# Final norm of an encoder trunk: token sums on output partitions, root and reciprocal on one column per 128 tokens

## The chip, the cores and the metric

One core of a Trainium2 chip runs the whole program. The metric is the device time of one execution in microseconds; of several runs the median is given. TensorE (PE) multiplies matrices into PSUM banks of 128 partitions x 512 fp32, VectorE (DVE), ScalarE (ACT) and GpSimd (POOL) work on 128 partitions, and SyncE (SP) issues most of the transfers.

## The reference

The reference is an encoder trunk with two layers over 1040 tokens (16 learned ones, 1024 given) of width 1024. Each layer has a norm, an input projection, a gated delta rule in both directions beside a short convolution, an output projection, a second norm and a SwiGLU network. Only its end matters here:

```python
def rmsnorm(x, w):
    xf = x.astype(jnp.float32)
    y = xf * lax.rsqrt(jnp.mean(xf * xf, axis=-1, keepdims=True) + RMS_EPS)
    return (y * w.astype(jnp.float32)).astype(x.dtype)
...
    h = rmsnorm(h, final_norm_w)
    return h[:, N_META:]
```

So every token is divided by the root of the mean square of its 1024 channels, and every channel is multiplied by a weight.

## The kernel before

Activations lie with channels on partitions: the residual is eight rows `hr[m]` of 128 channels x 1040 tokens, in two tiles `hb[0]` and `hb[1]` of four rows each. A sum over channels is therefore a sum over partitions and over the eight rows. Dense products are made in `dense`: for each chunk of tokens a PSUM bank takes three matmuls for each 128 channels of input (high and low parts of both operands), then an eviction runs, here `add_h`, which adds the bank to `hr[m]` on VectorE (line 905).

The last piece of the program is the rest of the last layer's down projection, with four blocks of input, so 12 matmuls for each product. It runs over three chunks of tokens, `FIN = [(16, 528), (528, 784), (784, 1040)]`, and inside a chunk over the eight rows. For each row there are the product and its eviction, `add_sq` (square on ScalarE, lines 181 and 187, sum over rows into `ss` on VectorE, line 188), and the multiplication by the norm's weight on ScalarE (line 1422). `ss`, whose tile is called `rstd` in the profile, then holds for each token and partition a sum over eight channels.

At the end of each chunk `finish_rstd` multiplies a matrix of ones with `ss` (line 196), so that every partition of bank `a` holds the full sum of each token, takes the root of the mean on ScalarE (line 197) and the reciprocal on VectorE (line 198), both over all tokens of the chunk on all 128 partitions. Then the eight rows are multiplied with the result (line 1426), the even ones on VectorE and the odd ones on GpSimd, and after every two rows SyncE issues a transfer to `out` (line 1427). The program ends with the last of these.

The products of this stage take their banks from `pwide`, which goes round `acc` (three banks) and `f` (two). Banks `a` (one) and `b` (two) are free for the norm. The order of the instructions on each engine is laid down when the program is built, by a planner that follows the order of the program text as a priority and puts later work ahead where it expects an engine to be free. On the chip each engine then runs its own queue in that order, with semaphores between engines.

Names that the change uses: `ident` is a 128x128 identity, `ones` a 128x128 matrix of ones, both fp32; `t2k` gives a tile of 128 x 4 x 128 fp32 from a ring of five; `bank("b")` gives a PSUM bank; `tt` is a product or sum of two tensors on VectorE, `ptt` the same on GpSimd; `st` is a ring of two small tiles, which the delta rule used before.

Of the kernel before, what the change touches and what calls it, by code (L numbers as in the profile page):

```python
# [7 lines left out]
F32 = mybir.dt.float32  # L8
F32R = mybir.dt.float32r
BF16 = mybir.dt.bfloat16  # L10
AF = mybir.ActivationFunctionType
ALU = mybir.AluOpType

DEPTH = 2
D = 1024
# [27 lines left out]
def trunk(ctx: ExitStack, tc: tile.TileContext, xT, w_in, w_ba, w_out, w_gu, w_dn,  # L43
          par_d, alog_d, dtb_d, cst_d, eye_d, out):
    nc = tc.nc
    sb = ctx.enter_context(tc.tile_pool(name="sb", bufs=1))
# [5 lines left out]
    def nm(p):  # L52
        cnt[0] += 1
        return f"{p}_{cnt[0]}"
# [4 lines left out]
    def row(tag, dt=F32, bufs=1):  # L59
        return sb.tile([128, L], dt, tag=tag, bufs=bufs, name=nm(tag))  # L60

    def t2k(tag):
        return sb.tile([128, 4, 128], F32, tag="ck2", bufs=5, name=nm(tag))
# [4 lines left out]
    def bank(tag):  # L68
        return psp.tile([128, 512], F32, tag=tag, bufs={"acc": 3, "a": 1, "f": 2, "b": 2}[tag], name=nm("p" + tag))
# [28 lines left out]
    mm = nc.tensor.matmul  # L98
    act = nc.scalar.activation
    tt = nc.vector.tensor_tensor  # L100
    stt = nc.vector.scalar_tensor_tensor
    ts = nc.vector.tensor_scalar
    ptt = nc.gpsimd.tensor_tensor
# [8 lines left out]
    ones = sb.tile([128, 128], F32, name="ones")  # L112
# [19 lines left out]
    def wload(src, nk):  # L132

        res = []
        step = min(nk, WK)
        for k0 in range(0, nk, step):
            kk = min(step, nk - k0)
            hi = wp.tile([128, WK, 128], F32R, tag="whi", name=nm("whi"))
            lo = wp.tile([128, WK, 128], F32R, tag="wlo", name=nm("wlo"))
            wsplit(src[:, k0:k0 + kk, :], hi[:, 0:kk, :], lo[:, 0:kk, :])  # L140
            for k in range(kk):
                res.append((hi[:, k, :], lo[:, k, :]))
        return res

    def dense(ws, xs, chunks, evac, pool=None):

        for (n0, n1) in chunks:
            n = n1 - n0
            ps = (pool or pacc)()
            K = len(xs)  # L150
            here = tc.cur_priority
            if mmp[0] is not None:
                at_prio(mmp[0])
            for k in range(K):
                (wh, wl), (xh, xl) = ws[k], xs[k]
                mm(ps[:, :n], wh, xh[:, n0:n1], start=(k == 0), stop=False)  # L156
                mm(ps[:, :n], wh, xl[:, n0:n1], start=False, stop=False)  # L157
                mm(ps[:, :n], wl, xh[:, n0:n1], start=False, stop=(k == K - 1))  # L158
            if mmp[0] is not None:
                mmp[0] = tc.cur_priority  # L160
                at_prio(here)
            here = tc.cur_priority
            if evp[0] is not None:
                at_prio(evp[0])
            evac(ps[:, :n], n0, n1)
            if evp[0] is not None:
                evp[0] = tc.cur_priority
                at_prio(here)
            for q in (jobs, jobs2, jobs3):
                f = q.pop(0) if q else None  # L170
                if f is not None:
                    f()
# [6 lines left out]
    def add_sq(h, ss, first, add=nc.vector.tensor_tensor, dve=False, prev=None):  # L179
        if first:  # L180
            after(act(out=ss, in_=h, func=AF.Square), prev)
        else:
            sq = c4k("sq")[:, 0:h.shape[1]]
            if dve:
                after(tt(out=sq, in0=h, in1=h, op=ALU.mult), prev)
            else:
                after(act(out=sq, in_=h, func=AF.Square), prev)
            add(out=ss, in0=ss, in1=sq, op=ALU.add)

    cols = {}  # L190

    def finish_rstd(ss, chunks):
        for j, (n0, n1) in enumerate(chunks):
            n = n1 - n0
            ps = bank("abb"[j])
            mm(ps[:, :n], ones, ss[:, n0:n1], start=True, stop=True)
            act(out=ss[:, n0:n1], in_=ps[:, :n], func=AF.Sqrt, scale=1.0 / D, bias=cols["eps"])
            nc.vector.reciprocal(out=ss[:, n0:n1], in_=ss[:, n0:n1])  # L198

    def finish_bc(ss, n0, n1, dst, ps=None):  # L200

# [25 lines left out]
    ss = row("rstd")  # L227
# [29 lines left out]
    ident = sb.tile([128, 128], F32, name="ident")  # L257
# [21 lines left out]
    for l in range(DEPTH):  # L279
# [607 lines left out]
        chunks = ochunks  # L887
        hb = [big(X[0][0]), big(X[0][1])]
        hr = [hb[m // 4][:, m % 4, :] for m in range(KT)]
# [13 lines left out]
        def add_h(m, then=None):  # L903
            def f(ps, n0, n1):
                tt(out=hr[m][:, n0:n1], in0=ps, in1=hr[m][:, n0:n1], op=ALU.add)
                if then is not None:
                    then(n0, n1)
            return f

        def next_norm(m, xm, wcol, ss):  # L910
            def f(n0, n1):
                split_scaled(hr[m][:, n0:n1], wcol, xm[0][:, n0:n1], xm[1][:, n0:n1])
                add_sq(hr[m][:, n0:n1], ss[:, n0:n1], m == 0)
            return f
# [25 lines left out]
        ss = row("rstd")  # L940
# [316 lines left out]
        for f in range(FT):  # L1257
# [21 lines left out]
            ps = {}  # L1279
# [63 lines left out]
        hr = [hb[m // 4][:, m % 4, :] for m in range(KT)]  # L1343
# [34 lines left out]
        for u, (p, b, m) in enumerate(UNITS):  # L1378
            if b == 1 and p in FIRST:
                dh, z = FIRST[p]  # L1380
                q = 4 * dh + m
# [12 lines left out]
            for j in range(NJ):  # L1394
                ps = bks[m, j]
                cs = slice(CW * j, CW * j + CW)
                for k in range(3):
                    th, tl = t_slot(3 * (u // 4) + k)
                    st = p in ("P2", "P5", "P1") and b == 0 and k == 0
# [4 lines left out]
                if b == NBK - 1:  # L1404
                    dh, z, op = TO[p]
# [5 lines left out]
        ss = row("rstd")  # L1411
        if not last:
            for m in range(KT):
                then = next_norm(m, x[m], par[:, (l + 1) * P_L + P_N1 + m:(l + 1) * P_L + P_N1 + m + 1], ss)
                dense(pre.pop(("dn", m)) if m < 2 else wload(w_dn[l, m, :, 0:NF, :], NF), rest, chunks, add_h(m, then), pwide)
                dma(hd[m], hr[m])
        else:
            for (n0, n1) in FIN:
                for m in range(KT):
                    dense(wds[m], rest, [(n0, n1)], add_h(m), pwide)  # L1420
                    add_sq(hr[m][:, n0:n1], ss[:, n0:n1], m == 0)
                    act(out=hr[m][:, n0:n1], in_=hr[m][:, n0:n1], func=AF.Copy, scale=par[:, 2 * P_L + m:2 * P_L + m + 1])
                finish_rstd(ss, [(n0, n1)])
                for m in range(0, KT, 2):
                    for q in (m, m + 1):
                        (tt, ptt)[q % 2](out=hr[q][:, n0:n1], in0=hr[q][:, n0:n1], in1=ss[:, n0:n1], op=ALU.mult)  # L1426
                    dma(out[m:m + 2, :, n0 - 16:n1 - 16].rearrange("m p t -> p m t"), hb[m // 4][:, m % 4:m % 4 + 2, n0:n1])
        if not last:
            finish_bc(ss, 0, L, rsd[1])
# [74 lines left out]
```

## Time and profile before

| | us |
|---|---|
| three runs | 2576.59, 2575.36, 2570.45 |
| median | 2575.36 |
| profiled execution, its own time | 2574.08 |
| its span on the core | 2572.3 |
| TensorE busy | 2493.8 |
| VectorE busy | 1722.1 |
| ScalarE busy | 1046.3 |
| GpSimd busy | 246.3 |

The span runs from the first to the last instruction on the core; the execution's own time is 1.8 us longer. The mean granted clock of TensorE over the span is 0.987 of full speed. In rows of the timeline stand the start, the duration, the engine, the line, the operation with the tiles that it writes and reads, the count, and in brackets the idle time of the engine before it with what ended it. Neighbouring instructions of one engine overlap by their fill and drain, so the distance of two starts is what an instruction costs in a row of equals.

### The profile page before, as it was taken

To read this page: it belongs to the slowest core of one execution; us is meant where nothing else is said; L and a number is where in the kernel's file an instruction comes from. 1 tells how busy PE (TensorE), PEld (TensorE's weight loads), DVE (VectorE), ACT (ScalarE), POOL (GpSimd) and SP (SyncE) were. 2 spreads that over 40 slices of the span, in tenths; PEclk is the share of its full clock that TensorE was granted. 3 is DMA by queue.
4 is the path that set the end of the run, shared out by engine and by line. 5 is a ranking of instruction groups with operands and counts; after the bars stand their busy time and mean duration, and the time that the engine had idled before them with its cause. 6 is when DMAs were issued, how large, how long until landed. Compare 5 with 4: busy or idle time off the path is not lost.

```text
span 2572.3 us, 44715 instructions
## 1 busy us (share of the span) xinstructions
PE 2493.8 (97%) x17442; PEld 2285.1 (89%) x17442; DVE 1722.1 (67%) x3055; ACT 1046.3 (41%) x1933; POOL 246.3 (10%) x264
## 2 busy tenths in 40 slices
PE   8989999999999999989999989999999999999997
PEld 6989999999999999989998878999888888887786
DVE  4678523549877777778656785235698767768866
ACT  5564323426333333434445633323453333334444
POOL 2041212200000000000011302222000000000002
PEclk9999999999999999999999999999999999999998
DMA  3458355524432222663323573456344222238431
GB/s 124 125 166 269 117 174 165 180 73 148 145 110 90 90 93 79 234 208 119 93 93 125 184 243 126 139 178 208 105 143 145 97 94 90 86 108 300 150 114 66
DMA packets 213567, 359.99 MB, mean 140 GB/s; under 512 B 25268, under 2 KB 87676, under 8 KB 213356
## 3 DMA queue, kind: packets, MB, share of 16 engines
q1 hardware_dynamic: 180684, 310.69, 36.8%
q10 hardware_dynamic: 30496, 42.09, 5.1%
q0 software_dynamic: 2176, 4.36, 0.6%
q8 instruction: 137, 2.24, 0.4%
q14 instruction: 74, 0.61, 0.1%
HBM read 266.60 MB, written 90.46 MB: 139 GB/s over the span
## 4 chain that ended last, share of the span: by engine, by line
PE 76%; DVE 9%; DMA 8%; issue 2%; ACT 2%; POOL 1%; ACTq 0%; SPq 0%; POOLq 0%; DVEq 0%
PE pacc L156 7%; PE pacc L158 7%; PE pacc L157 7%; PE pacc L1063 4%; PE pacc L1061 4%; PE pacc L1062 4%; PE pb L1063 3%; PE pb L1061 3%; PE pb L1062 3%; PE pf L1061 3%; PE pf L1063 3%; PE pf L1062 3%; PE pacc L1401 2%; PE pacc L1403 2%; PE pacc L1402 2%
## 5 line engine op out<-in xcount | busy, mean ns | idle before, releaser
L156 PE MATMUL pacc<-a,whi 128*128 128x346 f32 (+1 forms) x808 | 266.0, 332 | 14.2 <-ACT whi L129 9.6
L158 PE MATMUL pacc<-a,wlo 128*128 128x346 f32 (+1 forms) x808 | 266.4, 331 | 0.7 <-POOL wlo L130 0.7
L130 POOL TENSOR_TENSOR wlo<-raw,whi 128x512 fp32r<-128x512 f32 x92 | 123.1, 1340 | 1427.3 <-ACT whi L129 1357.1
L156 PE MATMUL pacc<-b,whi 128*128 128x346 f32 (+2 forms) x672 | 235.2, 351 | 0.5 <-DVE a L730 0.5
L158 PE MATMUL pacc<-b,wlo 128*128 128x346 f32 (+2 forms) x672 | 232.5, 348 | 1.0 <-DVE wlo L130 1.0
L157 PE MATMUL pacc<-a,whi 128*128 128x346 f32 (+1 forms) x688 | 227.0, 330 | 1.7 <-DVE a L900 1.7
L129 ACT ACTIVATE whi<-raw 128x512 fp32r<-128x512 f32 x168 | 105.2, 629 | 251.1 <-PE pacc L157 191.0
L157 PE MATMUL pacc<-b,whi 128*128 128x346 f32 (+2 forms) x580 | 201.5, 347 | 0.3 <-DVE b L900 0.3
L156 PEld LDWEIGHTS pacc<-a,whi 128*128 128x128 f32 x808 | 154.6, 192 | 19.8 <-ACT whi L129 10.7
L158 PEld LDWEIGHTS pacc<-a,wlo 128*128 128x128 f32 x808 | 155.8, 193 | 3.0 <-issue 1.5
L158 PEld LDWEIGHTS pacc<-b,wlo 128*128 128x128 f32 x672 | 126.9, 189 | 11.1 <-DVE wlo L130 1.3
L156 PEld LDWEIGHTS pacc<-b,whi 128*128 128x128 f32 x672 | 127.1, 189 | 10.4 <-issue 2.2
L157 PEld LDWEIGHTS pacc<-a,whi 128*128 128x128 f32 x688 | 132.0, 192 | 4.7 <-DVE a L900 2.0
L157 PEld LDWEIGHTS pacc<-b,whi 128*128 128x128 f32 x580 | 109.7, 189 | 8.8 <-issue 1.3
L1043 ACT ACTIVATE whi<-rw 128x512 fp32r<-128x512 f32 x92 | 58.1, 631 | 128.6 <-DVE rw L1271 29.8
L1043 ACT ACTIVATE b<-rw 128x512 fp32r<-128x512 f32 x64 | 40.2, 632 | 143.7 <-PE pacc L1062 47.3
L295 DVE TENSOR_TENSOR a<-pacc,rstd 128x346 f32<-128x346 f32 (+2 forms) x59 | 32.6, 553 | 83.7 <-PE pacc L158 83.6
L1426 POOL TENSOR_TENSOR b<-b,rstd 128x256 f32<-128x256 f32 (+1 forms) x12 | 13.3, 1137 | 726.2 <-DVE rstd L198 726.2
L1043 ACT ACTIVATE a<-rw 128x512 fp32r<-128x512 f32 x64 | 40.2, 629 | 101.6 <-PE pacc L1062 72.2
L295 DVE TENSOR_TENSOR b<-pacc,rstd 128x346 f32<-128x346 f32 (+1 forms) x63 | 32.2, 512 | 70.8 <-PE pacc L158 70.7
L1044 DVE TENSOR_TENSOR wlo<-rw,whi 128x512 fp32r<-128x512 f32 x92 | 62.9, 685 | 6.3 <-ACT whi L1043 5.6
L130 DVE TENSOR_TENSOR wlo<-raw,whi 128x512 fp32r<-128x512 f32 x76 | 52.3, 688 | 15.8 <-ACT whi L129 15.2
(969 smaller groups left out, 8041.7 us busy)
## 6 DMA issues: line engine op xcount, KB each, us to landing
raw<-in_w_in SPq DMA_DIRECT2D x112, 256.0 KB
raw<-in_w_gu SPq DMA_DIRECT2D x104, 256.0 KB
rw<-in_w_gu SPq DMA_DIRECT2D x88, 256.0 KB
rec<-aqd SPq DMA_DIRECT2D x62, 256.0 KB
rec<-vkd SPq DMA_DIRECT2D x61, 256.0 KB
rw<-in_w_dn SPq DMA_DIRECT2D x70, 192.0 KB
raw<-in_w_out SPq DMA_DIRECT2D x48, 256.0 KB
b<-ad SPq DMA_DIRECT2D x45, 260.0 KB
```

Source lines behind the costliest of these rows:

```text
L129: act(out=hi, in_=raw[:, 0:kk, :], func=AF.Copy)
L130: (tt if lov[0] else ptt)(out=lo, in0=raw[:, 0:kk, :], in1=hi.bitcast(F32), op=ALU.subtract)
L156: mm(ps[:, :n], wh, xh[:, n0:n1], start=(k == 0), stop=False)
L157: mm(ps[:, :n], wh, xl[:, n0:n1], start=False, stop=False)
L158: mm(ps[:, :n], wl, xh[:, n0:n1], start=False, stop=(k == K - 1))
L295: tt(out=t[:, n0:n1], in0=ps, in1=rstd[:, n0:n1], op=ALU.mult)
L1043: act(out=hi, in_=src, func=AF.Copy)
L1044: tt(out=lo, in0=src, in1=hi.bitcast(F32), op=ALU.subtract)
L1061: mm(ps[:, :CW], w[0][:, k, :], th[:, cs], start=first and k == 0, stop=False, skip_group_check=True)
L1062: mm(ps[:, :CW], w[0][:, k, :], tl[:, cs], start=False, stop=False, skip_group_check=True)
L1063: mm(ps[:, :CW], w[1][:, k, :], th[:, cs], start=False, stop=stop and k == nk - 1, skip_group_check=True)
L1401: mm(ps[:, :CW], wh[:, k, :], th[:, cs], start=st, stop=False, skip_group_check=True)
```

## The change

`finish_rstd` is replaced by `final_scale`. For each 128 tokens of the chunk a matmul takes the 128x128 block of `ss` as weights and one column of ones as the moving side; its output has the tokens on partitions and is one column of a bank, so a chunk has four columns or two. Root and reciprocal run on these columns. One product on VectorE of the identity with the columns, each spread over 128 places, gives for each 128 tokens a diagonal matrix, and a matmul with ones as weights spreads each diagonal over all partitions of a bank. All eight rows are then multiplied on VectorE with this bank, which stays in PSUM; GpSimd has no part any more. The transfers stay as they were.

```diff
-    def finish_rstd(ss, chunks):
-        for j, (n0, n1) in enumerate(chunks):
-            n = n1 - n0
-            ps = bank("abb"[j])
-            mm(ps[:, :n], ones, ss[:, n0:n1], start=True, stop=True)
-            act(out=ss[:, n0:n1], in_=ps[:, :n], func=AF.Sqrt, scale=1.0 / D, bias=cols["eps"])
-            nc.vector.reciprocal(out=ss[:, n0:n1], in_=ss[:, n0:n1])
+    def final_scale(ss, n0, n1):
+
+        nt = (n1 - n0) // 128
+        ps = bank("a")
+        for j in range(nt):
+            mm(ps[:, j:j + 1], ss[:, n0 + 128 * j:n0 + 128 * j + 128], ones[:, 0:1], start=True, stop=True)
+        r = sb.tile([128, 4], F32, tag="st", bufs=2, name=nm("rt"))[:, 0:nt]
+        act(out=r, in_=ps[:, 0:nt], func=AF.Sqrt, scale=1.0 / D, bias=cols["eps"])
+        nc.vector.reciprocal(out=r, in_=r)
+        dg = t2k("dg")[:, 0:nt, :]
+        tt(out=dg, in0=ident.unsqueeze(1).to_broadcast([128, nt, 128]), in1=r.unsqueeze(2).to_broadcast([128, nt, 128]), op=ALU.mult)
+        bc = bank("b")
+        for j in range(nt):
+            mm(bc[:, 128 * j:128 * j + 128], ones, dg[:, j, :], start=True, stop=True)
+        return bc[:, 0:n1 - n0]
...
-                finish_rstd(ss, [(n0, n1)])
+                bc = final_scale(ss, n0, n1)
                 for m in range(0, KT, 2):
                     for q in (m, m + 1):
-                        (tt, ptt)[q % 2](out=hr[q][:, n0:n1], in0=hr[q][:, n0:n1], in1=ss[:, n0:n1], op=ALU.mult)
+                        tt(out=hr[q][:, n0:n1], in0=bc, in1=hr[q][:, n0:n1], op=ALU.mult)
```

## The prediction

> **What bounds the kernel now.** I read the page first, then busy time by stretches for the tail, then the timeline of each engine there, because the change touches only the final norm and that lies in the last 40 us.
>
> ```profile
> span 2572.3 us, 44715 instructions
> PE 2493.8 (97%) x17442; PEld 2285.1 (89%) x17442; DVE 1722.1 (67%) x3055; ACT 1046.3 (41%) x1933; POOL 246.3 (10%) x264
> ...
> 2541.00:2548.00 7.00, 4.89 (x42) 4.69 (x41) 7.00 (x8) 1.55 (x4) 5.94 (x4) 1.00 0.56 217
> 2548.00:2556.00 8.00, 7.63 (x62) 7.38 (x62) 7.04 (x17) 6.71 (x17) 0.00 (x0) 1.00 0.20 74
> 2556.00:2561.00 5.00, 0.00 (x0) 0.00 (x0) 4.82 (x9) 1.80 (x4) 3.37 (x4) 0.67 0.53 177
> 2561.00:2564.50 3.50, 1.22 (x2) 0.50 (x2) 1.71 (x1) 0.53 (x2) 0.00 (x0) 0.50 0.14 47
> ```
>
> In the stretches the columns are length, busy PE, PEld, DVE, ACT and POOL, granted PE clock, DMA share and GB/s. Over the whole span TensorE is the bound (97%). In the tail it is not: from 2541 to 2548 VectorE is busy 7.00 of 7.00 us and TensorE only 4.89, and after 2556 TensorE has nothing left but the last sums. So the tail, some 35 us, is priced on VectorE and on the chain at its end.
>
> ```profile
> 2528.96 0.40 PE L158 MATMUL pacc<-b,a3f 128*128 128x512 f32 x1
> 2534.14 1.02 PE L196 MATMUL pa<-rstd,ones 128*128 128x512 f32 x2
> 2535.07 1.28 ACT L197 ACT_TABLE_LOAD   x1
> 2536.37 0.69 ACT L197 ACTIVATE rstd<-pa,epsc 128x512 f32<-128x512 f32 x1
> 2537.09 3.35 DVE L198 RECIPROCAL rstd<-rstd 128x512 f32<-128x512 f32 x1 [0.75 <-ACT rstd L197]
> 2541.30 6.19 DVE L1426 TENSOR_TENSOR b<-b,rstd 128x512 f32<-128x512 f32 x4
> 2547.88 0.39 PE L156 MATMUL pf<-b,a 128*128 128x256 f32 x1 [2.11 <-DVE b L905]
> 2551.72 0.59 PE L196 MATMUL pa<-rstd,ones 128*128 128x256 f32 x2
> 2554.24 1.75 DVE L198 RECIPROCAL rstd<-rstd 128x256 f32<-128x256 f32 x1
> 2555.36 0.28 PE L158 MATMUL pacc<-b,a3f 128*128 128x256 f32 x1
> 2556.52 3.21 DVE L1426 TENSOR_TENSOR b<-b,rstd 128x256 f32<-128x256 f32 x4
> 2559.65 0.41 DVE L905 TENSOR_TENSOR b<-pacc,b 128x256 f32<-128x256 f32 x1
> 2559.98 0.98 DVE L188 TENSOR_TENSOR rstd<-rstd,sq 128x256 f32<-128x256 f32 x2
> 2561.02 1.22 PE L196 MATMUL pa<-rstd,ones 128*128 128x256 f32 x2 [5.39 <-DVE rstd L188]
> 2562.28 0.47 ACT L197 ACTIVATE rstd<-pa,epsc 128x256 f32<-128x256 f32 x1 [1.23 <-PE pa L196]
> 2562.79 1.75 DVE L198 RECIPROCAL rstd<-rstd 128x256 f32<-128x256 f32 x1 [1.82 <-ACT rstd L197]
> 2564.57 3.01 DVE L1426 TENSOR_TENSOR b<-b,rstd 128x256 f32<-128x256 f32 x4
> 2564.62 3.55 POOL L1426 TENSOR_TENSOR b<-b,rstd 128x256 f32<-128x256 f32 x4 [5.17 <-DVE rstd L198]
> ```
>
> Three costs are to be read here. The first chunk's reciprocal (3.35) and four multiplications (6.19) block VectorE for most of 10.4 us; TensorE runs out of free banks and waits 2.11 us at 2547.88 for an eviction (L905). The last dense matmul is over at 2555.64 (2555.36 + 0.28), but its eviction starts only at 2559.65, because the second chunk's reciprocal and multiplications stand ahead of it on VectorE. And from the last eviction (over at 2560.06) the chain square, add, sums, root, reciprocal, multiplications is serial; the last multiplication ends at 2568.17 and the span at 2572.3, 4.1 us later.
>
> **The sums.** Each sum over the channels was one matmul with ones as weights and 512 or 256 columns. Now the sums are weights, 128 tokens at a time, with one moving column: four or two such matmuls. The nearest rows have weights of 128x128 and 36 to 72 columns, in the same two passes.
>
> ```profile
> 83.66 0.31 PE L387 MATMUL pb<-g,utri 128*128 128x36 f32 x2
> 83.80 0.39 PE L387 MATMUL pb<-g,ltri 128*128 128x36 f32 x2
> 84.02 0.42 PE L388 MATMUL pb<-g,ones 128*128 128x72 f32 x2
> 84.25 0.41 PE L158 MATMUL pacc<-a,wlo 128*128 128x348 f32 x1
> 2535.13 0.28 PE L157 MATMUL pf<-b,a 128*128 128x256 f32 x1
> ```
>
> Starts are 0.14 to 0.23 us apart, so four take 0.6 to 0.9; the one of 512 columns held TensorE from 2534.14 to 2535.13, 0.99. I book nothing here (bounds -0.4 to 0).
>
> **Root and reciprocal.** They now run over four or two elements per partition.
>
> ```profile
> L867 ACT ACTIVATE st<-st x17: 204/206/226, 460.4 to 1839.1; 128x4 f32<-128x4 f32 x16, 16x4 f32<-16x4 f32 x1
> L868 DVE RECIPROCAL st<-st x17: 164/178/179, 460.7 to 1839.4; 128x4 f32<-128x4 f32 x16, 16x4 f32<-16x4 f32 x1
> L869 DVE TENSOR_TENSOR a3f<-a3f,st x8: 678/692/2267, 1763.0 to 1839.6; 128x512 f32<-128x512 f32 x8
> ```
>
> The root falls from 0.69 or 0.47 to 0.21, the reciprocal from 3.35 or 1.75 to 0.18. The table load of 1.28 stays where it is. The scaled identity is new on VectorE: 0.69 for 512 columns (the product with a broadcast column, L869), about 0.42 for 256 (as L905).
>
> **The spread.** Its matmuls, ones against the scaled identity, have as many columns in all as the old sums: 0.99 for the first chunk and, from 2551.72, about 0.5 for the second. In the last chunk the old sums took 1.22 with the clock at 0.50, against 0.59 at 1.00, so I book 1.25 there. The clock fell during the idle of TensorE: a mean of 0.67 over 2556 to 2561 means that it was at half for 3.3 of the 5.0 us, so from about 2557.7, some 2.05 us after the last dense matmul; the idle of 2.11 before 2547.88 left it at 1.00. The Trainium skill (TensorE: Matmul & The Clock Gate, "What's actually happening") gives half rate after an idle window of about 3.4 us, in windows that run freely. The trace agrees that idleness halves the clock, and its 2.05 us was enough. By that rule a last chain that starts within a window of the last matmul would run at full rate, and this chunk's spread would take 0.6 and its sums 0.6.
>
> **The multiplications.** All eight are on VectorE now, with one operand in PSUM and GpSimd silent.
>
> ```profile
> L1426 POOL TENSOR_TENSOR b<-b,rstd x12: 777/906/1751, 2540.6 to 2567.3; 128x256 f32<-128x256 f32 x8, 128x512 f32<-128x512 f32 x4
> 2477.02 0.68 DVE L1407 TENSOR_TENSOR b<-pa,b 128x512 f32<-128x512 f32 x1
> 2477.62 0.55 DVE L1182 TENSOR_TENSOR wlo<-rw,whi 128x384 fp32r<-128x384 f32 x1
> 2548.08 0.41 DVE L905 TENSOR_TENSOR b<-pacc,b 128x256 f32<-128x256 f32 x1
> 2548.41 0.41 DVE L905 TENSOR_TENSOR b<-pf,b 128x256 f32<-128x256 f32 x1
> ```
>
> Beside GpSimd four on VectorE took 6.19 (1.55 each). A product from PSUM, back to back, has its successor start after 0.60 (2477.02 to 2477.62) and, at 256 columns, 0.33 (2548.08 to 2548.41). Eight are 4.8 and 2.7: halving the engines is a gain, since each was slowed by the other. VectorE's block for the first chunk goes from 3.35 + 6.19 = 9.54 to 0.18 + 0.69 + 4.8 = 5.7.
>
> **The sum.** TensorE: the wait of 2.11 goes, since five banks hold five products of 1.4 to 1.5 us (12 matmuls each; 62 took 7.63) and the block is 5.7; the spreads add 1.0 + 0.5. The last dense matmul then ends at 2555.64 - 2.11 + 1.5 = 2555.0. Its eviction is over at 2555.5, and with the old 0.90 from there through square and add (2560.06 to 2560.96) the sums are ready at 2556.4 instead of 2560.96: 4.6 us earlier at best. What is late next is the second chunk's scale. Its spread needs root, reciprocal and identity first, two hops more than before, and in the old order its multiplications came between the last two evictions; I expect them behind the last eviction. Ahead of the last add they hold it for the rest of 2.7 us: only 2.4 earlier. Behind that add they hold the last reciprocal, which is not ready before 2556.4 + 1.28 + 0.26 = 2557.9, until 2559.1, a loss of 1.2: 3.4 earlier. The last chain: root -0.24, reciprocal -1.57, identity +0.46, spread +1.25, end after the first multiplication -0.7. That last term is bounded by -0.85 (eight multiplications end at 2.7 instead of 3.55) and by -0.5 if the writes set the pace:
>
> ```profile
> L1427 SPq DMA_DIRECT2D out<-b x12: 372/372/395, 2542.5 to 2568.2; - x12
> 2568.20:2572.30 4.10, 0.00 (x0) 0.00 (x0) 0.00 (x0) 0.00 (x0) 0.00 (x0) 0.50 0.38 129
> ```
>
> The last is issued at 2568.2, and 4.1 follow, which stay. The chain gives -0.8; with -2.4 or -3.4 the whole is -3.2 or -4.2, middle -3.7. The profiled execution took 2574.08 (span 2572.3 and 1.8 around it), which is 1.3 below the median of 2575.36; -3.7 makes 2570.4 from the one and 2571.7 from the other, and I say 2571.0.
>
> **Rivals.** (A) The second chunk's scale comes early enough, in the shadow of the third chunk's matmuls; VectorE had that room once its block is 4 us shorter, and against it speaks that its sums stood late in TensorE's queue (2551.72). Then -4.6 - 0.8 = -5.4, and with the clock still full -6.7: 2567.4 to 2570. (B) The forecast. (C) Eight multiplications on one engine, at a stretch, still starve TensorE: VectorE's queue is in order, and evictions of both later chunks wait behind 4.8 us. For it: the same row of 2.11 today, with a block that was interrupted twice for evictions; against it, the shorter block. If the wait stays whole, -3.7 + 2.1 = -1.6: 2573.1. (D) Slower: the spread matmuls stand in TensorE's in-order queue directly behind the sums and hold the dense matmuls of the next chunk while root, reciprocal and identity run. In the first chunk that is table load 1.28, root 0.25, reciprocal 0.2, identity 0.7 and hops, 2.6 us; in the second 0.95. That eats up the 3.7; it decides when the clock falls too, since one product of 1.4 us at half rate then loses 1.4, two lose 2.8: +2.7, 2577. For it: nothing forces the queue to put work between; against it, the old queue put the first sums 4.8 us behind the chunk's last product (2528.96 + 0.40 to 2534.14), so the order leaves room.
>
> **How the numbers follow.** B 0.48, A 0.30, C 0.13, D 0.09. About 0.3%, 7.7 us, is what a measurement can tell from no change; the three runs spread over 6.1. Only A's end, -6.7, comes near it, and the scatter of medians can carry it over: faster 0.17. D lies at +2.7 and needs as much scatter again: slower 0.04. The rest, 0.79, is within it. The range takes in A's end less one microsecond of scatter, 2566.5, and most of D, 2576.5.
>
> **What would show it.** Right: no GpSimd work in the tail; reciprocals of 0.18; eight products of 0.6 or 0.33 on VectorE at a stretch; no wait of TensorE near 2547; the last dense matmul ending near 2555, the last add near 2556.4 to 2558.6, the span near 2568.6. Wrong: a wait of TensorE for the scaled identity (D), a wait for an eviction (C), products from PSUM slower than 0.4 at 256 columns, or writes that land over 4.1 us after the last multiplication.

## The result and the profile after

The change took the median from 2575.12 us (14 runs, 2567.97 to 2580.71) to 2568.12 (14 runs, 2565.01 to 2572.94). The ratio of after to before is 0.9979 with a 95% interval of 0.9969 to 0.9988, that is some 5.4 us less (3.1 to 8.0). A second series (e9, the change once more) gave 0.9969 (0.9958 to 0.9981).

The profiled execution has a span of 2569.1 us against 2572.3. These 3.2 us do not measure the change: the start of the first chunk's last eviction, which lies ahead of anything that the change touches, came at 2529.39 before and at 2531.43 after, and over all the profiled executions below it lay between 2524.5 and 2534.4. Up to it the traces before and after hold the same numbers of instructions (17246 matmuls, 3008 on VectorE, 1895 on ScalarE, 252 on GpSimd). So I measure the **tail**, from the start of that eviction to the end of the span.

The timeline of VectorE, before and after (start, duration, engine, line, operation; `b<-pacc,b 128x512` is the eviction):

```profile
2529.39 0.69 DVE L905 TENSOR_TENSOR b<-pacc,b 128x512 f32<-128x512 f32 x1 [0.67 <-PE pacc L158]
```

```profile
2531.43 0.69 DVE L913 TENSOR_TENSOR b<-pacc,b 128x512 f32<-128x512 f32 x1 [0.67 <-PE pacc L158]
...
2538.70 0.18 DVE L200 RECIPROCAL rt<-rt 128x4 f32<-128x4 f32 x1 [1.69 <-ACT rt L199]
2538.91 0.69 DVE L202 TENSOR_TENSOR dg<-ident,rt 128x512 f32<-128x512 f32 x1
...
2542.86 4.87 DVE L1434 TENSOR_TENSOR b<-pb,b 128x512 f32<-128x512 f32 x8
...
2556.27 0.42 DVE L913 TENSOR_TENSOR b<-pacc,b 128x256 f32<-128x256 f32 x1
2556.72 2.74 DVE L1434 TENSOR_TENSOR b<-pb,b 128x256 f32<-128x256 f32 x8
2559.38 0.42 DVE L188 TENSOR_TENSOR rstd<-rstd,sq 128x256 f32<-128x256 f32 x1
2560.78 0.17 DVE L200 RECIPROCAL rt<-rt 128x2 f32<-128x2 f32 x1 [0.99 <-ACT rt L199]
2560.98 0.43 DVE L202 TENSOR_TENSOR dg<-ident,rt 128x256 f32<-128x256 f32 x1
2562.72 2.74 DVE L1434 TENSOR_TENSOR b<-pb,b 128x256 f32<-128x256 f32 x8 [1.31 <-PE pb L205]
```

The tail is 2572.3 - 2529.39 = 42.9 before and 2569.1 - 2531.43 = 37.7 after: 5.2 us less, which agrees with the ratio. Where they went is read from busy time in two stretches, up to the last add (L188) and behind it; the first row of each pair is the longer one. Before:

```profile
2529.39:2560.96 31.57, 24.13 (x196) 23.19 (x194) 26.60 (x42) 16.83 (x37) 9.74 (x8) 0.95 0.26 94
2560.96:2572.30 11.34, 1.22 (x2) 0.50 (x2) 4.77 (x6) 0.57 (x2) 3.55 (x4) 0.50 0.33 108
```

After:

```profile
2531.43:2559.80 28.37, 25.25 (x216) 25.06 (x214) 21.78 (x52) 16.33 (x37) 0.00 (x0) 1.00 0.25 91
2559.80:2569.10 9.30, 1.83 (x8) 1.45 (x8) 3.34 (x10) 0.26 (x1) 0.00 (x0) 0.59 0.52 175
```

Up to the last add 31.57 became 28.37 (3.2 less): VectorE has 4.8 us less to do there, GpSimd nothing, and TensorE 1.1 more. Behind the add 11.34 became 9.30 (2.0 less). TensorE's timeline shows that the wait at 2547.88 is gone, and the order that holds the end:

```profile
2536.17 0.95 PE L197 MATMUL pa<-ones,rstd 128*128 128x1 f32 x8
2536.98 0.36 PE L156 MATMUL pf<-b,a 128*128 128x256 f32 x1
...
2540.72 1.05 PE L205 MATMUL pb<-dg,ones 128*128 128x128 f32 x8
2541.53 0.36 PE L157 MATMUL pf<-b,a 128*128 128x256 f32 x1
...
2555.95 0.28 PE L158 MATMUL pacc<-b,a3f 128*128 128x256 f32 x1
2556.07 0.61 PE L205 MATMUL pb<-dg,ones 128*128 128x128 f32 x4
2559.85 0.61 PE L197 MATMUL pa<-ones,rstd 128*128 128x1 f32 x4 [3.17 <-DVE rstd L188]
2561.47 1.22 PE L205 MATMUL pb<-dg,ones 128*128 128x128 f32 x4 [1.01 <-DVE dg L202]
```

The second chunk's spread stands behind the last dense matmul, so its eight products (2556.72, 2.74 us) stand behind the last eviction and ahead of the last add. That is the first of the two orders in the forecast, the one in which the products hold the last add.

### The profile page after: what moved, and what is told of

The parts are those of the page before. It is cut to its first block, busy times and chain, and to the rows that moved or that the text cites. A ratio compares the mean times of both kernels' runs of the same rounds, so it can differ in the third digit from the quotient of the medians.

```text
span 2569.1 us, 44758 instructions
## 1 busy us (share of the span) xinstructions
PE 2500.2 (97%) x17468; PEld 2291.3 (89%) x17468; DVE 1716.6 (67%) x3070; ACT 1045.9 (41%) x1933; POOL 233.6 (9%) x252
## 4 chain that ended last, share of the span: by engine, by line
PE 79%; DVE 8%; DMA 7%; issue 2%; ACT 2%; POOL 1%; ACTq 0%; SPq 0%; DVEq 0%; POOLq 0%
PE pacc L156 7%; PE pacc L158 7%; PE pacc L157 7%; PE pacc L1071 4%; PE pacc L1070 4%; PE pacc L1069 4%; PE pf L1069 3%; PE pf L1071 3%; PE pf L1070 3%; PE pb L1071 3%; PE pb L1069 3%; PE pb L1070 3%; PE pacc L1411 2%; PE pacc L1409 2%; PE pacc L1410 2%
## 5 line engine op out<-in xcount | busy, mean ns | idle before, releaser
L158 PEld LDWEIGHTS pacc<-b,wlo 128*128 128x128 f32 x672 | 126.9, 189 | 10.7 <-issue 1.3
L156 PEld LDWEIGHTS pacc<-b,whi 128*128 128x128 f32 x672 | 127.0, 189 | 10.1 <-issue 2.2
L1069 PE MATMUL pacc<-b,whi 128*128 128x260 f32 (+1 forms) x172 | 53.1, 309 | 0.0
```

The costliest lines, as they stand in the source:

```text
L1069: mm(ps[:, :CW], w[0][:, k, :], th[:, cs], start=first and k == 0, stop=False, skip_group_check=True)
```

## The experiments

Every tail is the end of the span less the start of the eviction, from the profile of that kernel. It is split at the end of the last add. Each stands for one execution. Three kernels were profiled twice: the change agreed within 0.1 us, and two others differed by 0.5 and 0.4, which lay in the clock of TensorE behind the last add, as shown below.

| kernel | tail | up to the last add | behind it |
|---|---|---|---|
| before | 42.9 | 31.6 | 11.3 |
| the change | 37.7 | 28.4 | 9.3 |
| new scale, products divided (e1) | 42.9 | 31.4 | 11.5 |
| old scale, products on VectorE (e2) | 39.7 | 29.6 | 10.1 |
| new in the last chunk alone (e3) | 41.4 | 31.6 | 9.8 |
| new in the first two chunks alone (e4) | 39.2 | 28.4 | 10.8 |
| spread twice (e5) | 40.3 | 29.7 | 10.7 |
| products placed by hand (e6) | 36.1 | 27.3 | 8.9 |
| GpSimd beside the last products (e7) | 38.4 | 28.4 | 10.1 |
| five products from the bank, three on GpSimd (e8) | 37.5 | 27.9 | 9.7 |

**One part each: the scale or the products.**

e1, in place of the change's products:

```diff
-                bc = final_scale(ss, n0, n1)
+                act(out=ss[:, n0:n1], in_=final_scale(ss, n0, n1), func=AF.Copy)
...
-                        tt(out=hr[q][:, n0:n1], in0=bc, in1=hr[q][:, n0:n1], op=ALU.mult)
+                        (tt, ptt)[q % 2](out=hr[q][:, n0:n1], in0=hr[q][:, n0:n1], in1=ss[:, n0:n1], op=ALU.mult)
```

> The new scale, but copied from its bank to SBUF on ScalarE, and the products divided between VectorE and GpSimd as before. Measure: the tail, from the start of the first chunk's last eviction on VectorE to the end of the span; 42.9 us before, 37.7 after. Theory (both parts carry: the shorter reciprocal and the quicker products): VectorE's first block is 0.18 + 0.69 + 6.2 = 7.1 instead of 9.5, the copy costs about 0.45 in the last chain and GpSimd's products bring its end back to 7.7 after the first of them: tail 40.5 to 41.5. Rival 1 (only the move of the products off GpSimd carries): tail 42.5 to 43.5. Rival 2 (only the reciprocal carries): 37.7 to 38.5.

e2, in the kernel before:

```diff
-                        (tt, ptt)[q % 2](out=hr[q][:, n0:n1], in0=hr[q][:, n0:n1], in1=ss[:, n0:n1], op=ALU.mult)
+                        tt(out=hr[q][:, n0:n1], in0=hr[q][:, n0:n1], in1=ss[:, n0:n1], op=ALU.mult)
```

> The old scale with its long reciprocals, but all eight products on VectorE, both operands in SBUF. Theory: products of 512 columns fall from 1.55 to 0.60 without GpSimd beside them, so VectorE's first block is 3.35 + 4.8 = 8.2 instead of 9.5, TensorE's wait shrinks from 2.1 to about 0.9, and after the first product of the last chunk the end is nearer by about 1.3: tail 38.5 to 40. Rival 1 (products carry all): 37.7. Rival 2 (reciprocal carries all): 41.5 to 43.

Moving the products alone (e2) took the tail to 39.7, as the theory said, and the ratio to 0.9982 (0.9970 to 0.9993). Its eight products take 4.89 us, 0.60 each, with both operands in SBUF and GpSimd idle, and TensorE's wait for an eviction shrinks from 2.11 to 0.82:

```profile
2541.58 4.89 DVE L1426 TENSOR_TENSOR b<-b,rstd 128x512 f32<-128x512 f32 x8
```

```profile
2546.87 0.39 PE L156 MATMUL pf<-b,a 128*128 128x256 f32 x1 [0.82 <-DVE b L905]
```

The new scale alone, with its copy (e1), gave nothing: tail 42.9, ratio 1.0004 (0.9995 to 1.0014). That is rival 1's number, and my 40.5 to 41.5 was a miss. Yet rival 1 as a whole is wrong too, since the products alone leave 2.0 of the 5.2 us. VectorE and TensorE in e1 show why:

```profile
2541.85 5.78 DVE L1434 TENSOR_TENSOR b<-b,rstd 128x512 f32<-128x512 f32 x4 [0.60 <-ACT rstd L1431]
...
2555.99 3.02 DVE L1434 TENSOR_TENSOR b<-b,rstd 128x256 f32<-128x256 f32 x4
2558.94 0.94 DVE L188 TENSOR_TENSOR rstd<-rstd,sq 128x256 f32<-128x256 f32 x1
2559.80 0.41 DVE L913 TENSOR_TENSOR b<-pacc,b 128x256 f32<-128x256 f32 x1
```

```profile
2548.02 0.38 PE L156 MATMUL pf<-b,a 128*128 128x256 f32 x1 [0.99 <-DVE b L913]
```

Four products beside GpSimd take 5.78 and VectorE waits 0.60 for the copy, so TensorE still waits 0.99 for an eviction. In this order the second chunk's products come ahead of the last eviction, and even the add behind them is stretched to 0.94, as GpSimd still works. What the reciprocal gave was spent on the copy, the spread and that order. How much of it was order and how much the copy, e1 does not tell.

**One place each: the last chunk or the first two.** e3 takes the new scale and products where `n1 == L` and the old ones elsewhere; e4 where `n1 < L`:

```diff
-                bc = final_scale(ss, n0, n1)
+                if n1 == L:
+                    bc = final_scale(ss, n0, n1)
+                else:
+                    finish_rstd(ss, [(n0, n1)])
```

> The new scale and products in the last chunk alone; the first two chunks as before. Theory: the change gains in two places, 3.2 us up to the last add (through the first two chunks' blocks) and 2.0 in the chain behind it, of which 0.65 by a clock that was still full. Here only the second is left, with the clock at half for the sums: tail 41.0 to 41.6. Rival (the last chain carries all): 37.7 to 38.5.

> The new scale and products in the first two chunks alone; the last as before. Theory: the 3.2 us up to the last add stay, and with the clock still full the last sums take 0.6 instead of 1.2: tail 39.0 to 39.8. Rival (the last chain carries all): 42.5 to 43.

Both came out inside the theory: 41.4 and 39.2, that is 1.5 and 3.7 less than before, 5.2 together. The ratios agree for e4 (0.9983, 0.9974 to 0.9993); for e3 1.0006 (0.9994 to 1.0019) cannot tell 1.5 us from nothing. TensorE's last sums, first in e3, then in e4:

```profile
2566.05 1.01 PE L197 MATMUL pa<-ones,rstd 128*128 128x1 f32 x4 [5.39 <-DVE rstd L188]
```

```profile
2556.82 0.70 PE L212 MATMUL pa<-rstd,ones 128*128 128x256 f32 x2 [3.17 <-DVE rstd L188]
```

The 0.5 that e4 gains behind the last add is the clock: its old sums take 0.70 instead of 1.22. In e3 the new sums take 1.01 at half clock, where the change took 0.61. So the greater part, 3.2 us up to the last add, lies in the first two chunks, and it is reached at the end of the third, where the last eviction no longer waits.

**The price of the spread.** Every spread matmul is issued twice:

```diff
-        for j in range(nt):
+        for j in 2 * list(range(nt)):
             mm(bc[:, 128 * j:128 * j + 128], ones, dg[:, j, :], start=True, stop=True)
```

> The change, with every spread matmul issued twice. Tail after the change 37.7 us. Theory (TensorE is the bound up to its last dense matmul once VectorE's blocks are short, and all of the last chain is serial): the first chunk's second spread adds 0.8, the second chunk's 0.5, the last one's 1.2 at half clock, so 2.0 to 2.6: tail 39.7 to 40.3. Rival (the first two chunks' spreads lie in the shadow of VectorE): only 1.2: tail 38.8 to 39.0.

```profile
2537.95 1.95 PE L205 MATMUL pb<-dg,ones 128*128 128x128 f32 x16
...
2554.19 1.05 PE L205 MATMUL pb<-dg,ones 128*128 128x128 f32 x8
2558.40 1.01 PE L197 MATMUL pa<-ones,rstd 128*128 128x1 f32 x4 [3.16 <-DVE rstd L188]
2560.42 2.08 PE L205 MATMUL pb<-dg,ones 128*128 128x128 f32 x8 [1.01 <-DVE dg L202]
```

The tail is 40.3, 2.6 more, at the top of the theory's range: 1.3 up to the last add and 1.4 behind it. The ratio to the kernel before is 0.9992 (0.9978 to 1.0005). Up to the last add the first chunk's doubled spread costs 0.9 (1.95 against 1.05) and the second chunk's 0.4 (1.05 against 0.61), as the theory had it: they are not hidden any more, and up to its last dense matmul TensorE is the bound. Behind the add the spread costs 0.9, not 1.2. Another 0.4 is no price of the spread: after an idle of 3.16 us, as long as in the change, the sums took 1.01 instead of 0.61. The top of the range was reached by luck.

**What stands ahead of the last add.** The products of the first two chunks are placed behind adds of later rows (chunk, row: products as chunk, row), each with an order dependency on that add:

```diff
+PLACE = {(1, 6): [(0, 0)], (1, 7): [(0, 1), (0, 2)], (2, 0): [(0, 3), (0, 4)], (2, 1): [(0, 5)], (2, 2): [(0, 6)], (2, 3): [(0, 7), (1, 0)],
+         (2, 4): [(1, 1), (1, 2)], (2, 5): [(1, 3), (1, 4)], (2, 7): [(1, 5), (1, 6), (1, 7)],
+         "end": [(2, q) for q in range(8)]}
...
+                    for k, q in PLACE.get((c, m), ()):
+                        product(k, q, adds[c, m])
```

> The change, with the products of the first two chunks placed by hand: one or two behind the add of each later row, the last three behind the last add, where VectorE waits for sums and root anyway. Nothing is left out. Theory: what stands ahead of the last add after the change is the second chunk's block of eight products (2.7 us), so the last add comes 1.7 earlier, and the last spread may still find the full clock (0.6): tail 35.3 to 36.0. Rival (the products cost VectorE the same wherever they stand, and the writes to memory then close up at the end): 37.3 to 38.

The tail is 36.1, just above my range. The last add came 1.1 us earlier, not 1.7: the second chunk's spread now stands ahead of the last dense matmul, which ends 25.3 us after the mark instead of 24.8. Once more, beside the change on one chip:

> The products placed by hand once more, beside the change on the same chip. Theory: tail 36.1 again, 1.6 us below the change; in the ratio that is 0.0006, which these rounds can hardly tell. Rival (the shorter tail is a matter of the clock's window in one execution): tail 36.7 or more.

There it is 36.6, nearly what the rival said. Up to the last add both executions have the same 27.3, 1.1 less than the change; behind it they differ by 0.5, and TensorE's timeline shows by what. The first execution, then the second:

```profile
2552.17 0.61 PE L200 MATMUL pa<-ones,rstd 128*128 128x1 f32 x4 [2.04 <-DVE rstd L191]
2553.82 0.71 PE L208 MATMUL pb<-dg,ones 128*128 128x128 f32 x4 [1.04 <-DVE dg L205]
```

```profile
2553.39 0.61 PE L200 MATMUL pa<-ones,rstd 128*128 128x1 f32 x4 [2.04 <-DVE rstd L191]
2555.04 1.22 PE L208 MATMUL pb<-dg,ones 128*128 128x128 f32 x4 [1.04 <-DVE dg L205]
```

The idle times are equal, 2.04 and 1.04, and the spread takes 0.71 once and 1.22 the other time. So 1.1 us of the shorter tail belong to the order and up to 0.5 to the phase of the clock. The ratios are 0.9980 (0.9971 to 0.9989) and 0.9972 (0.9960 to 0.9985), on the second chip beside 0.9969 for the change: a gain of 0.0004 to 0.0006 is too small for these series, and I do not call this version faster.

**GpSimd beside products from a bank.** Six products on GpSimd are added beside the last chunk's end; `fdg[0]` is the scaled identity, and nothing uses their result:

```diff
+                if n1 == L:
+                    junk = t2k("jk")
+                    for q in range(6):
+                        ptt(out=junk[:, 0:2, :], in0=fdg[0], in1=fdg[0], op=ALU.mult)
```

> The change, with six products of 128x256 on GpSimd beside the last chunk's spread and products; their result is not used. Theory 1: a VectorE product with one operand in PSUM is not slowed by GpSimd: the eight stay at 0.33 each. Rival 1: they go to 0.75, the rate of the kernel before, and the tail grows by 2 or more. Theory 2: GpSimd's closing drain ends some 3.4 us after its last product, so the end comes about 1 us later than without it: tail 38.4 to 39. Rival 2: the drain costs nothing: 37.7.

```profile
2559.67 2.74 DVE L1441 TENSOR_TENSOR b<-pb,b 128x256 f32<-128x256 f32 x8 [1.31 <-PE pb L208]
```

```profile
2558.58 4.07 POOL L1438 TENSOR_TENSOR jk<-dg 128x256 f32<-128x256 f32 x6 [731.70 <-DVE dg L205]
```

Both first theories hold: eight products still take 2.74, and the tail is 38.4. The sums (0.61) and the spread (1.22) are as in the change, so the 0.7 us more are not the clock. The closing instructions show what they are, first of the kernel before, then of e7, e4, the change and e2 (duration in ns: least, median and greatest; then first and last start in us):

```profile
L1499 POOLq DRAIN  x3: 40/102/6937, 2564.6 to 2572.0; - x3
L1499 SPq DRAIN  x3: 7/7/7, 2570.7 to 2571.8; - x3
```

```profile
L1514 POOLq DRAIN  x3: 40/102/4007, 2562.0 to 2566.5; - x3
L1514 SPq DRAIN  x3: 7/7/7, 2565.3 to 2566.3; - x3
```

```profile
L1521 POOLq DRAIN  x3: 40/102/6452, 2560.3 to 2567.3; - x3
L1521 SPq DRAIN  x3: 7/7/7, 2566.0 to 2567.1; - x3
```

```profile
L1507 SPq DRAIN  x3: 7/7/7, 2568.3 to 2568.6; - x3
L1507 POOLq DRAIN  x2: 40/71/102, 2568.6 to 2568.9; - x2
```

```profile
L1499 SPq DRAIN  x3: 7/7/7, 2568.5 to 2568.8; - x3
```

GpSimd's long drain ends at 2564.6 + 6.9 = 2571.5 before and at 2566.0 in e7, 3.4 us behind its last product in both (2568.17 and 2562.65). SyncE's first drain, which I take for the moment when it has seen the last writes land, comes 0.8 and 0.7 earlier, at 2570.7 and 2565.3. In all five kernels the end follows 0.8 to 0.9 behind the later of the two; in the change and in e2, with no GpSimd work in the last chunk, that is SyncE's drain. So the end of the kernel before waited for GpSimd, not for the writes: from SyncE's first drain to the end it was 1.6, and in the change it is 0.8.

**GpSimd with a share again.** In the first two chunks it takes three of the eight products, from a copy:

```diff
+                if n1 < L:
+                    act(out=ss[:, n0:n1], in_=bc, func=AF.Copy)
...
-                        tt(out=hr[q][:, n0:n1], in0=bc, in1=hr[q][:, n0:n1], op=ALU.mult)
+                        if n1 < L and q in (1, 4, 6):
+                            ptt(out=hr[q][:, n0:n1], in0=ss[:, n0:n1], in1=hr[q][:, n0:n1], op=ALU.mult)
+                        else:
+                            tt(out=hr[q][:, n0:n1], in0=bc, in1=hr[q][:, n0:n1], op=ALU.mult)
```

> The change, but in the first two chunks GpSimd makes three of the eight products from a copy of the bank that ScalarE makes, while VectorE makes five from the bank. Theory: with an operand in PSUM VectorE is not slowed (0.60 and 0.33 each), so the blocks shrink to 3.0 and 1.65; the first was hidden already, and the second stands ahead of the last eviction or the last add: tail 36.5 to 37.7. Rival (the two engines slow one another as before the change): 39 to 40.5.

```profile
2540.87 3.08 DVE L1439 TENSOR_TENSOR b<-pb,b 128x512 f32<-128x512 f32 x5 [0.60 <-ACT rstd L1433]
...
2552.99 1.74 DVE L1439 TENSOR_TENSOR b<-pb,b 128x256 f32<-128x256 f32 x5
2554.64 0.74 DVE L188 TENSOR_TENSOR rstd<-rstd,sq 128x256 f32<-128x256 f32 x1
2555.31 0.41 DVE L913 TENSOR_TENSOR b<-pacc,b 128x256 f32<-128x256 f32 x1
```

Five products take 3.08 beside GpSimd, 0.62 each, so the bank keeps them apart; the tail is 37.5. Its order is that of e1, with the products ahead of the last eviction, yet it needs 27.9 up to the last add where e1 needed 31.4. That is what products from the bank are worth, with five of the eight on VectorE instead of four. The add behind them, with both operands in SBUF, is stretched to 0.74. Its ratio was 0.9971 (0.9962 to 0.9980), the lowest of its series, so it ran again beside the change:

> Five products on VectorE from the bank and three on GpSimd in the first two chunks, once more, beside the change on the same chip. Its time before was the lowest (ratio 0.9971) though its tail of 37.5 is only 0.2 us below the change. Theory: that lead was scatter: a ratio within 0.0006 of the change's here. Rival (the version gains outside the tail): again 0.001 below the change.

> The change itself once more, beside the two versions below on one chip. Theory: what it gains lies after the start of the first chunk's last eviction, so the tail is 37.7 again (37.5 to 37.9) whatever the whole span does, and the ratio to the kernel before is 0.998. Rival (part of the gain lies ahead of the tail): a tail near 37.7 with a ratio further from 1 than 5.2 us explain, under 0.997.

The change gave 37.7 again with 0.9969, this version 37.1 with 0.9979 (0.9966 to 0.9991): the order of the two ratios turned round. The lead was scatter. The two tails of this version, 37.5 and 37.1, differ by the clock: after the same idle of 2.66 us the sums took 0.93 and 0.61, and the spread 1.22 and 1.12. The change's 0.9969 is 8 us, more than its tail explains, and just the figure of the rival. Its interval (0.9958 to 0.9981) holds the 5.2 too, so the ratio does not decide; against the rival stands that up to the mark the executed instructions are the same in number.

## Why the prediction was right or wrong

The forecast, 2571.0 and within 0.3%, stands: 2568.12 is in the range, and the ratio's 5.4 us are under 7.7. That alone says little, since the old median of 2575.36 lies in the range as well; the tail and its parts are the test. The mechanism was B, as named: TensorE's wait went, and the second chunk's products stood behind the last eviction and held the last add. But B promised 3.7, and the tail gave 5.2. By its steps:

- Products, reciprocal, identity: 4.87 and 2.74 for eight (4.8 and 2.7), 0.18 to 0.15 (0.18), 0.69 and 0.43 (0.69 and 0.42). Right. The root took 0.26 instead of 0.21.
- Sums and spread of the first chunk: 0.81 each from start to the next matmul (2536.17 to 2536.98, 2540.72 to 2541.53); I had booked 0 and 1.0 beside sums of 0.99, so each is 0.2 cheaper. The second spread, booked at 0.5 ahead of the last dense matmul, stands behind it. The marks lie 2.04 us apart, so in the times of the kernel before the last dense matmul ends at 2556.23 - 2.04 = 2554.2, where I had 2555.0. That is the first term that was mis-sized, 0.8 us: the last add came 3.2 earlier, not 2.4.
- The chain behind the last add: 2.0 less, not 0.8. Of the missing 1.2 the sums are 0.6 (0.61 against 1.22), where I had booked nothing. They still found the full clock, after 3.17 us of idle, where I had taken it at half. At half clock the new sums take 1.01 (e3, e5), so the clock gave 0.4 and the one moving column 0.2. The 0.4 are luck: in e5 an idle of 3.16 had already halved the clock.
- The rest is the end. From the first product to the end of the span it was 7.73, and is 6.38: 1.35 less, where I had booked 0.7 and 0.85 as the outer bound. Up to SyncE's first drain it was 6.1 and is 5.6, about the 0.5 that I gave for the case that the writes set the pace. The bound was wrong, because I took the 4.1 us behind the last write's issue for a fixed close. Some 0.7 to 0.8 of them were GpSimd's drain, which goes when GpSimd has no work near the end (e7, e2).

Rival A, with 0.30, did not come in, but its saving up to the add can be had in part: up to the last add it promised 4.6, the change has 3.2 and e6, by hand, 4.3. C and D did not occur: TensorE shows no wait for an eviction and none for a scaled identity ahead of the last chunk. The argument that two engines slowed each other was the strongest of the prediction, and e2 and e8 bear it out. What the prediction did not say is that the parts do not add up: 3.2 for the products alone, nothing for the new scale with a copy, 5.2 together. I read the bank as the link between them: it holds the spread where VectorE can read it without a copy and without GpSimd in its way. That is argued: no run has the new scale with a copy and all eight products on VectorE, so the price of the copy alone is not shown.

The Trainium skill (TensorE: Matmul & The Clock Gate, "What's actually happening") lets its windows run freely. With that the traces agree: an idle of 3.17 us left the clock full after the change and one of 3.16 halved it in e5, and two executions of e6 with equal idle times differ. Its idle window of about 3.4 us they do not bear out as a least idle time, since 2.05 us were enough before. One number for "how long TensorE may idle" cannot be taken from one trace.

## What to carry to other kernels

Before dividing elementwise work between VectorE and GpSimd, look at what each product costs alone: here eight on VectorE took 4.87 where four beside GpSimd's four took 6.19, and an operand left in PSUM kept VectorE free of GpSimd altogether. A per-column quantity that is equal on all partitions is dear to compute on all of them (a reciprocal of 3.35 against 0.18), but its spread back costs matmuls that become visible once TensorE is the bound again. When a change gains at the end of a program, measure from a mark just ahead of it: everything before that mark moved by 10 us between executions, twice the effect.

## What the runs showed of the hardware that was not expected

- GpSimd's closing drain ended 3.3 to 3.4 us behind its last product in four kernels (before, e1, e4 and e7) and held the program's end 0.7 to 0.8 us beyond SyncE's first drain.
- Products on VectorE with one operand in PSUM kept their pace beside GpSimd (2.74 for eight in e7, 3.08 for five in e8), while sums with both operands in SBUF went from 0.42 to 0.74 and 0.94. The Trainium skill (SBUF — State Buffer, "SBUF: two separate sides") describes a port pair that VectorE needs for two SBUF inputs and shares with GpSimd as an exclusive lock; the traces agree with that as far as the PSUM operand goes.
- The same spread, after the same idle of 1.04 us, took 0.71 and 1.22 in two executions of one program. The same sums took 0.61 after 3.17 us of idle in the change and 1.01 after 3.16 in e5.
